# Pass order and operand placement in a split-precision matmul kernel: mirrored passes for the second output tile, second parts one k tile on

## The chip, the cores and the metric

The kernel runs on one core of one Trainium2 chip, as one launch. The metric is device microseconds from the start to the end of an execution; three runs of the kernel before were timed. A profile of one further execution gives each instruction with its start, its end and what it waited for.

## The reference

The reference is two layers of a hybrid block over 256 tokens with 16 learned tokens ahead of them (272 in all), width 1024, in float32. Each layer normalizes, projects to twelve groups of columns, runs three mixers (retention, a gated linear recurrence, differential attention), joins them with gates, and adds a convolutional feed-forward part. A last normalization ends it.

```python
def mixer(hn, w_in, w_branch, w_out, lb, lam_p, subln_g, lambda_init, valid, pos):
    proj = (hn @ w_in).astype(F32)
    rq, rk, rv, rg, hq, hf, hi, hg, dq, dk, dv, mg = jnp.split(proj, offs, axis=-1)
    o_ret = retention(rq, rk, rv, rg, valid, pos)
    o_hg = hgrn2(hq, hf, hi, hg, lb, valid)
    o_da = diff_attention(dq, dk, dv, lam_p, subln_g, lambda_init, valid, pos)
    branches = jnp.stack([o_ret, o_hg, o_da], axis=2)
    y_b = jnp.einsum('blnc,ncd->blnd', branches, w_branch)
    y = jnp.sum(jax.nn.sigmoid(mg) * y_b, axis=2)
    return y @ w_out

def conv_ffn(hn, w_ffn_in, conv_w, conv_b, w_ffn_out, valid):
    u = jnp.where(valid[None, :, None], hn @ w_ffn_in, 0.0)
    up = jnp.pad(u, ((0, 0), (CONV_W - 1, 0), (0, 0)))
    c = conv_b + sum(conv_w[j] * up[:, j:j + l] for j in range(CONV_W))
    gate, val = jnp.split(c, 2, axis=-1)
    return (jax.nn.silu(gate) * val) @ w_ffn_out

for li in range(2):
    h = h + mixer(rms_norm(h, norm_mix_g[li]), ...)
    h = h + conv_ffn(rms_norm(h, norm_ffn_g[li]), ...)
return rms_norm(h, norm_final_g)[:, PAD:]
```

Nearly all arithmetic is in the matrix products with `w_in`, `w_branch`, `w_out`, `w_ffn_in` and `w_ffn_out`.

## The kernel before, in words

**Tiles.** Activations lie with features on the 128 partitions and tokens along the free axis: 272 columns in layer 0, and 258 in most of layer 1 (`t0` = 14 drops tokens that nothing reads any more; the six projections in `FULL` keep 272). Weights are cut on the host into tiles of 128 x 128, in the order of use, and eight tiles make a chunk, `CHUNK_TILES`. A product (`products`, L850) makes two output tiles, `f` = 0 and 1, over the k tiles of its operand: 8, or 22 for `fo`. The k tile is the outer loop and `f` the inner one.

**Two parts.** To get float32 precision out of the single-pass matmul type, every operand is split: `hi` is the operand rounded to that type, `lo` is the rest. A weight tile meets an activation tile in three passes, each a weight load and a matmul into the same PSUM accumulator:

```python
nc.tensor.matmul(o, wh, hi, start=first, stop=False)
nc.tensor.matmul(o, wh, lo, start=False, stop=False)
nc.tensor.matmul(o, wl, hi, start=False, stop=last)
```

These are L873, L874 and L875 of the profile. The weights' split is made on the chip, chunk by chunk, in `_Weights.next` (L577): a DMA from SP's queue brings `wraw`, ScalarE (ACT) writes `whi`, VectorE (DVE) writes `wlo` as the difference. The activations' split is made by `Norm.take` and `Norm.next` (the `x` tiles), by `split_blocks` (`b0` to `b2`), and by `split` (`y` for `wo`, `g` for `fo`).

**Stages.** Names in `ORDER` are projections (`rq` to `m2`, products with `w_in`), `b0` to `b2` (`w_branch`), `wo`, `fi` (`w_ffn_in`, 22 pairs) and `fo`. A pair of output tiles over 8 k tiles is 16 weight tiles and 48 passes. Projections and `fi` stream the `x` tiles, the others stream tiles that lie in slots, buffers of four k tiles each (`SLOTS` of them). In layer 1 `fo` is computed the other way round (`final`, L1351): the weights stream, 512 columns at a time, and the activations are loaded.

**Order.** Everything is recorded first (`_Plan.add`) with a cost and a due time; `_Plan.order` then simulates the engines and buffers, and each engine's instructions are issued in that order. The products keep their program order; small matmuls of the mixers go between them.

**Places.** Addresses within a partition are chosen by hand. `_places` (L127) gives each weight tile its place inside its chunk's buffers, the same in `whi` and `wlo`, by a wanted byte offset modulo `LINE`, 256: 0 for projections in layer 0 (`APART`), 96 for those with 258 columns, another place for every `fi` pair (`SPREAD`), and 64 more for each k tile for `b0` to `b2`, `wo` and `fo`, whose slots hold k tiles 1088 bytes apart. The `x` tiles lie 320 columns (`WIDE`), 1280 bytes, apart, so that all k tiles have the same offset modulo 256. `_runs` turns the places of a chunk into as few ACT and DVE instructions as it can.

Of the kernel before, what the change touches and what calls it, by code (L numbers as in the profile page):

```python
# [11 lines left out]
F32 = mybir.dt.float32  # L12
# [25 lines left out]
SLOTS = 13  # L38
# [47 lines left out]

def _turns(li):

    pairs = [x for x in ORDER if x[0][0] not in MARKS]
    if li == DEPTH - 1:
        pairs = [x for x in pairs if x[0] != "fo"]
    groups = [[x] for x in pairs]
    if li == 0:
        groups[:2] = [pairs[:2]]
    turned = [[x] for n in (BASE, ("fi",)) for x in [x for x in pairs if x[0] in n][DEFER - 1 : DEFER]]
    out = []
    for group in groups:  # L100
        if group == [("fo", 3)]:
            out.append([("fo", 3, k, f) for f in range(2) for k in range(FK)])
        else:
            nk = _ktiles(group[0][0])
            out.append([x + (k, f) for k in range(nk // 2) for x in group for f in range(2)])
            out[-1] += [x + (k, f) for x in group for k in range(nk // 2, nk) for f in range(2)]
# [11 lines left out]
APART = (0, 96)  # L118
# [4 lines left out]
SPREAD = [16 * i for i in range(16)] + [8 + 40 * i for i in range(6)]  # L123
WIDE = 320


def _places(depth=DEPTH):  # L127

    wants = []
    for li in range(depth):
        for name, j, k, _ in sum(_turns(li), []):
            if name == "fo" and (li == DEPTH - 1 or j == 3):
                wants.append(None)
                continue
            short = li == DEPTH - 1 and name not in FULL
            if name in BASE or name == "fi":
                wants.append((SPREAD[j] + 4 * T0 * short if name == "fi" else APART[short]) % LINE)
                continue  # L140
            wants.append(APART[short] + BLOCK * (name[0] == "b" or name in ("wo", "fo")) + 64 * (k % 4))
    out = []
    for c in range(0, len(wants), CHUNK_TILES):
        at, places = 0, []
        for want in wants[c : c + CHUNK_TILES]:
            if want is not None:
                at += (want // 4 - at) % (LINE // 4)
            places.append(at)
            at += P
        assert at <= ROOM  # L150
        out.append(places)
    return out


def _runs(places):


    runs = []
    for i, at in enumerate(places):
        if runs and at == runs[-1][1] + runs[-1][2] * P:  # L160
            runs[-1][2] += 1
        else:
            runs.append([i, at, 1])
    out = []
    for i, at, n in runs:
        if out and out[-1][4] == n and (out[-1][3] == 1 or at == out[-1][1] + out[-1][2] * out[-1][3]):
            if out[-1][3] == 1:
                out[-1][2] = at - out[-1][1]
            out[-1][3] += 1
        else:  # L170
            out.append([i, at, 0, 1, n])
    return out
# [22 lines left out]
def _stream(w_in, w_branch, w_out, w_ffn_in, w_ffn_out):  # L195
# [17 lines left out]
    out = out.reshape(n, CHUNK_TILES, P, P).transpose(0, 2, 1, 3)  # L213
# [349 lines left out]
class _Weights:  # L563
# [9 lines left out]
    def part(self, t, at, step, runs, n):  # L573

        return bass.AP(t.tensor, t.offset + at, [list(t.ap[0]), [max(step, 1), runs], [1, n * P]])

    def next(self):  # L577
        c, i = divmod(self.used, CHUNK_TILES)
        self.used += 1
        if i == 0:  # L580
# [7 lines left out]
            for p in range(pieces):  # L588
                n = CHUNK_TILES // pieces
                cols = slice(p * n * P, (p + 1) * n * P)  # L590
                self.sp.dma_start(raw[:, cols], self.w[c][:, cols])
                for first, at, step, runs, each in _runs(self.places[c][p * n : (p + 1) * n]):
                    src = raw[:, (p * n + first) * P : (p * n + first + runs * each) * P].rearrange("p (r x) -> p r x", r=runs)
                    self.act.activation(self.part(hi, at, step, runs, each), src, AF.Copy)
                    self.dve.tensor_tensor(out=self.part(lo, at, step, runs, each), in0=src, in1=self.part(hi, at, step, runs, each).bitcast(F32), op=SUB)
            self.plan.key = due
            self.cut = hi, lo
        hi, lo = self.cut
        at = self.places[c][i]
        return hi[:, at : at + P], lo[:, at : at + P]  # L600
# [16 lines left out]
def _trace(ctx, tc, plan, a, depth, probe):  # L617
# [232 lines left out]
    def products(xs, name, j, t0=0):  # L850
# [14 lines left out]
        for _, i, k, f in tiles:  # L865
            hi, lo = (x[:, t0:] for x in xs(k))
            begun = left[i, f] < _ktiles(name)
            left[i, f] -= 1
            plan.key = clock[0]
            wh, wl = weights.next()  # L870

            def run(o=to[i, f], wh=wh, wl=wl, hi=hi, lo=lo, first=not begun, last=left[i, f] == 0):
                nc.tensor.matmul(o, wh, hi, start=first, stop=False)  # L873
                nc.tensor.matmul(o, wh, lo, start=False, stop=False)  # L874
                nc.tensor.matmul(o, wl, hi, start=False, stop=last)  # L875

            plan.main.append(plan.add("pe", run, cost, [to[i, f]], [wh, wl, hi, lo]))
            clock[0] += cost
# [26 lines left out]
    def split(hi, lo, x):  # L905
        act.activation(hi, x, AF.Copy)
        tt(lo, x, hi.bitcast(F32), SUB)
# [29 lines left out]

    def split_blocks(name, blocks, t0):

        his, los = [], []  # L940
        for x in blocks:
            hi, lo = slot4(name + "hi", F32R), slot4(name + "lo", F32R)
            split(hi[:, :, t0:], lo[:, :, t0:], x[:, :, t0:])
            his.append(hi)
            los.append(lo)
        return lambda k: (his[k // 4][:, k % 4, :], los[k // 4][:, k % 4, :])

    for li in range(depth):
# [402 lines left out]
        def final():  # L1351
# [21 lines left out]
            for k, t, c in order:  # L1373
# [5 lines left out]
                gh, gl = (x[k // 4][:, k % 4, tokens(t)] for x in (hi, lo))  # L1379
# [27 lines left out]
        for name, j in ORDER:  # L1407
# [88 lines left out]
            elif name in ("b0", "b1", "b2"):  # L1496
# [5 lines left out]
                else:  # L1502
                    tt(g, ps, g, MUL)
                    tt(yy, yy, g, ADD)
                    if name == "b2":
# [3 lines left out]
                        split(st["yhi"][j // 2][:, two, t0:], st["ylo"][j // 2][:, two, t0:], yy)  # L1509
            elif name == "wo":  # L1510
                hi, lo = st["yhi"], st["ylo"]
                ps = products(lambda k: (hi[k // 4][:, k % 4, :], lo[k // 4][:, k % 4, :]), name, j, t0)
# [7 lines left out]
            elif name == "fi":  # L1520
                ps = products(lambda k: x_tile(k, norm.folded), name, j, t0)
                if j % 4 == 0:
                    st.setdefault("ghi", []).append(slot4("ghi", F32R))
                    st.setdefault("glo", []).append(slot4("glo", F32R))
# [4 lines left out]
                first = META if last else 0  # L1529
# [12 lines left out]
                split(st["ghi"][j // 4][:, j % 4, first:], st["glo"][j // 4][:, j % 4, first:], c[:, 0, :])  # L1542
# [3 lines left out]
            else:  # L1546
                hi, lo = st["ghi"], st["glo"]
                ps = products(lambda k: (hi[k // 4][:, k % 4, :], lo[k // 4][:, k % 4, :]), name, j)
# [34 lines left out]
```

## Time and profile before

| | |
|---|---|
| time, median of 3 runs (lowest to highest) | 1326.98 us (1326.49 to 1327.44) |
| the profiled execution: its own time, and its span | 1326.42 us, 1324.6 us |
| mean granted TensorE clock | 0.999 |
| matmuls, weight loads: busy time | 1314.0 us, 1285.7 us |
| DVE, ACT: busy time | 962.4 us, 816.4 us |
| `wraw` loads on SP's queue | 402 of 512 KB and 4 of 256 KB |
| `whi` conversions on ACT, `wlo` on DVE | 408 and 408 |

Times in the profile are microseconds from the span's start, durations of one instruction are nanoseconds. A matmul's row has its start and the time until its result is through the array; since passes overlap, a stream's speed is the distance between starts, not that duration. A row of the timeline has start, duration, engine, line, operation, output<-inputs, and shape.

### The profile page before, as it was taken

What the parts mean: (1) busy time and instruction counts of PE and PEld (TensorE: products, weight loads), DVE (VectorE), ACT (ScalarE), POOL (GpSimd) and SP (SyncE); (2) the same over time, 40 slices, a digit from 0 to 9 for tenths busy, and PEclk for the clock granted to TensorE, in tenths of its full rate; (3) what the DMA queues carried; (4) which work ended last, traced back from release to release, by engine and by line L of the source; (5) the groups of instructions that cost most, each with busy time, mean ns of one, the idle gap of its engine ahead of it and who ended that gap; (6) DMA issues with size and microseconds to landing.
All of it is one profiled execution on the core that took longest, in us unless ns stands there. A gap on an engine that the chain in (4) does not pass through costs nothing.

```text
span 1324.6 us, 28929 instructions
## 1 busy us (share of the span) xinstructions
PE 1314.0 (99%) x11862; PEld 1285.7 (97%) x11862; DVE 962.4 (73%) x1630; ACT 816.4 (62%) x1374; POOL 83.2 (6%) x161
## 2 busy tenths in 40 slices
PE   9999999999999999999999999999999999999998
PEld 8999999999999999999999999999999999999986
DVE  7675777697585789886574757776985867898753
ACT  6847454756576566666456475547565865766643
POOL 5000000001010020000030000000011100200000
PEclk9999999999999999999999999999999999999999
DMA  7544543444544545555555445444445345365653
GB/s 272 194 150 153 172 148 132 140 144 139 181 143 152 183 144 183 183 170 181 175 176 187 149 159 173 148 144 144 148 140 183 136 165 201 131 211 185 204 182 107
DMA packets 60755, 219.07 MB, mean 165 GB/s; under 512 B 6864, under 2 KB 6992, under 8 KB 60624
## 3 DMA queue, kind: packets, MB, share of 16 engines
q1 hardware_dynamic: 60336, 216.71, 48.0%
q8 instruction: 93, 1.52, 0.5%
q10 hardware_dynamic: 288, 0.52, 0.1%
q14 instruction: 38, 0.31, 0.1%
HBM read 216.16 MB, written 1.05 MB: 164 GB/s over the span
## 4 chain that ended last, share of the span: by engine, by line
PE 95%; DVE 3%; ACT 1%; issue 0%; DMA 0%; SPq 0%; DVEq 0%
PE main L873 28%; PE main L875 27%; PE main L874 27%; PE fo L1383 2%; PE fo L1385 2%; PE fo L1384 2%; PE lev L1064 1%; DVE two_b L558 1%; PE ds L1248 1%; PE ms L558 1%; PE do L558 1%; PE ro L558 1%; PE ho L558 1%; PE vt L558 1%; DVE wlo L558 1%; PE s L558 0%
## 5 line engine op out<-in xcount | busy, mean ns | idle before, releaser
L873 PE MATMUL main<-xh,whi 128*128 128x272 f32 (+1 forms) x2368 | 691.8, 292 | 0.7 <-ACT whi L558 0.7
L875 PE MATMUL main<-xh,wlo 128*128 128x272 f32 (+1 forms) x2368 | 676.1, 286 | 1.0 <-DVE wlo L558 0.9
L874 PE MATMUL main<-xl,whi 128*128 128x272 f32 (+1 forms) x2368 | 675.7, 285 | 1.3 <-DVE xl L558 1.3
L558 DVE TENSOR_TENSOR wlo<-wraw,whi 128x1024 fp32r<-128x1024 f32 (+1 forms) x408 | 497.2, 1223 | 197.9 <-ACT whi L558 195.2
L558 ACT ACTIVATE whi<-wraw 128x1024 fp32r<-128x1024 f32 (+1 forms) x408 | 426.4, 1048 | 228.1 <-PE main L874 160.1
L873 PEld LDWEIGHTS main<-xh,whi 128*128 128x128 f32 x2368 | 446.1, 188 | 2.6 <-ACT whi L558 1.1
L874 PEld LDWEIGHTS main<-xl,whi 128*128 128x128 f32 x2368 | 446.1, 188 | 2.3 <-DVE xl L558 1.7
L875 PEld LDWEIGHTS main<-xh,wlo 128*128 128x128 f32 x2368 | 445.7, 188 | 2.4 <-DVE wlo L558 2.3
L558 DVE SCALAR_TENSOR_TENSOR two_b<-main,small,two_b 128x256 f32<-128x256 f32 (+2 forms) x144 | 65.4, 489 | 30.7 <-ACT two_b L558 29.0
L558 ACT ACTIVATE two_b<-main,small 128x272 f32<-128x272 f32 (+1 forms) x72 | 37.2, 566 | 29.6 <-PE main L875 29.6
L558 POOL TENSOR_TENSOR y<-h,rstd 128x272 f32<-128x272 f32 x32 | 34.5, 1113 | 317.7 <-ACT rstd L558 317.7
L875 PE MATMUL main<-ghi,wlo 128*128 128x272 f32 x176 | 51.0, 290 | 0.0
L873 PE MATMUL main<-ghi,whi 128*128 128x272 f32 x176 | 50.9, 289 | 0.0
L874 PE MATMUL main<-glo,whi 128*128 128x272 f32 x176 | 50.2, 285 | 0.0
L558 ACT ACTIVATE vsrc<-main 128x544 f32<-128x544 f32 x24 | 15.0, 625 | 38.5 <-PE main L875 38.4
L873 PE MATMUL main<-b0hi,whi 128*128 128x272 f32 (+1 forms) x128 | 38.2, 298 | 0.0
L873 PE MATMUL main<-b1hi,whi 128*128 128x272 f32 (+1 forms) x128 | 38.1, 298 | 0.0
L875 PE MATMUL main<-b2hi,wlo 128*128 128x272 f32 (+1 forms) x128 | 36.7, 286 | 0.0
L875 PE MATMUL main<-yhi,wlo 128*128 128x272 f32 (+1 forms) x128 | 36.7, 286 | 0.0
L875 PE MATMUL main<-b1hi,wlo 128*128 128x272 f32 (+1 forms) x128 | 36.6, 286 | 0.0
L875 PE MATMUL main<-b0hi,wlo 128*128 128x272 f32 (+1 forms) x128 | 36.6, 286 | 0.0
L873 PE MATMUL main<-b2hi,whi 128*128 128x272 f32 (+1 forms) x128 | 36.5, 285 | 0.0
(244 smaller groups left out, 1934.4 us busy)
## 6 DMA issues: line engine op xcount, KB each, us to landing
wraw<-in_w SPq DMA_DIRECT2D x402, 512.0 KB, 3.3
h<-in_h SPq DMA_DIRECT2D x4, 272.0 KB, 5.7
dec<-in_dec SPq DMA_DIRECT2D x2, 544.0 KB, 5.5
wraw<-in_w SPq DMA_DIRECT2D x4, 256.0 KB, 5.4
const<-in_const SPq DMA_DIRECT2D x1, 937.0 KB, 6.4
gain<-in_gl SPq DMA_DIRECT2D x1, 512.0 KB, 5.2
out<-y ACTq DMA_DIRECT2D x2, 256.0 KB, 2.8
out<-y SPq DMA_DIRECT2D x2, 256.0 KB, 2.7
```

The costliest lines, as they stand in the source:

```text
L558: self.plan.add(self.name, lambda: f(*args, **kw), cost, outs, ins, args[2] if method == "activation" else None)
L873: nc.tensor.matmul(o, wh, hi, start=first, stop=False)
L874: nc.tensor.matmul(o, wh, lo, start=False, stop=False)
L875: nc.tensor.matmul(o, wl, hi, start=False, stop=last)
L1064: nc.tensor.matmul(o, keys, x, start=True, stop=True)
L1248: nc.tensor.matmul(ss[m][:, at : at + nk], q[half, hd, q0 : q0 + P], k[half, hd, :nk], start=True, stop=True)
L1383: nc.tensor.matmul(o, gh, wh, start=False, stop=False)
L1384: nc.tensor.matmul(o, gl, wh, start=False, stop=False)
L1385: nc.tensor.matmul(o, gh, wl, start=False, stop=end)
```

## The change

Six things are changed together.

- **Pass order.** For the second output tile of a k tile (`odd`), the pass `wl`·`hi` comes first instead of last. So the passes of a k tile go hi, lo, hi for the first output tile and hi, hi, lo for the second.
- **Second parts one place on.** The `lo` part of k tile k lies in place (k + 1) % 4 of its tile, for `x` and for every slot. Writes of several k tiles that wrap are made in two pieces (`split`).
- **`x` tiles 272 columns apart** instead of 320 (`WIDE` is gone), so k tiles lie 64 bytes on from each other modulo 256, as in the slots.
- **Weight places.** `_places` gives `whi` and `wlo` places of their own: 64 bytes more per k tile in every stage, one offset for all stages of a width (`APART` is now 64 and 160 bytes, counted from the streamed operand), the second part's place by the operand of the pass that runs before its load. `SPREAD` is gone. Within a chunk the odd tiles are stored first; the host permutes the stream to match.
- **Conversions.** `_boxes` replaces `_runs`: an ACT and a DVE instruction write up to a two-level box of tiles. By the new placement 388 of 404 chunks still take one instruction an engine; ten chunks of `fo` in layer 0 take four, one takes six, five (the first two chunks among them) two.
- **Slots.** 14 instead of 13. In layer 1 the `g` tiles lie 256 columns apart.

```diff
-SLOTS = 13
+SLOTS = 14
...
-APART = (0, 96)
+GROUPED = 4 * KD
+BEGIN = 64
...
-SPREAD = [16 * i for i in range(16)] + [8 + 40 * i for i in range(6)]
-WIDE = 320
+APART = (64, 160)
...
-        for name, j, k, _ in sum(_turns(li), []):
-            if name == "fo" and (li == DEPTH - 1 or j == 3):
+        for i, (name, j, k, _) in enumerate(sum(_turns(li), [])):
+            if name == "fo" and li == DEPTH - 1:
                 wants.append(None)
                 continue
             short = li == DEPTH - 1 and name not in FULL
-            if name in BASE or name == "fi":
-                wants.append((SPREAD[j] + 4 * T0 * short if name == "fi" else APART[short]) % LINE)
-                continue
-            wants.append(APART[short] + BLOCK * (name[0] == "b" or name in ("wo", "fo")) + 64 * (k % 4))
+            apart = APART[short] + 4 * T0 * short - BEGIN + BLOCK * (name not in BASE and name != "fi")
+            turn = 4 * T * (k % 4)
+            lo = apart + turn if i % 2 == 0 else before
+            wants.append([apart + turn, lo + 4 * T * (i % 2 == 0 and len(wants) >= GROUPED)])
+            before = apart + turn
...
+        if c >= GROUPED and None not in mine:
+            order = [i for i in order if i % 2] + [i for i in order if not i % 2]
+            by = [sorted(order, key=lambda i: i ^ 1)] * 2
+            if any(b[0] - a[0] not in (0, 4 * T) for a, b in zip(mine, mine[1:])):
+                by = [sorted(order, key=lambda i: mine[i][part] % LINE) for part in range(2)]
+                order = by[0]
...
+                for first, outer, inner, dims in _boxes(*mine):
+                    src = self.part(raw, (p * n + first) * P, inner * P, P, outer, inner)
+                    to_hi, to_lo = (self.part(t, *x, outer, inner) for t, x in zip((hi, lo), dims))
+                    self.act.activation(to_hi, src, AF.Copy)
+                    self.dve.tensor_tensor(out=to_lo, in0=src, in1=to_hi.bitcast(F32), op=SUB)
...
-    xs = [[fixed([P, KD // 2, WIDE], f"x{n}{i}", F32R)[:, :, :T] for n in "hl"] for i in range(3)]
+    xs = [[fixed([P, KD // 2, T], f"x{n}{i}", F32R) for n in "hl"] for i in range(3)]
...
-        return tuple(t[:, k % 4, :] for t in xs[1 if k >= 4 else 2 if folded else 0])
+        return tuple(t[:, (k + n) % 4, :] for n, t in enumerate(xs[1 if k >= 4 else 2 if folded else 0]))
...
-                nc.tensor.matmul(o, wh, hi, start=first, stop=False)
-                nc.tensor.matmul(o, wh, lo, start=False, stop=False)
-                nc.tensor.matmul(o, wl, hi, start=False, stop=last)
+                passes = [(wh, hi), (wh, lo)]
+                passes.insert(0 if odd else 2, (wl, hi))
+                for n, (w, x) in enumerate(passes):
+                    nc.tensor.matmul(o, w, x, start=first and n == 0, stop=last and n == 2)
...
-    def split(hi, lo, x):
+    def split(hi, lo, x, k):
+
         act.activation(hi, x, AF.Copy)
-        tt(lo, x, hi.bitcast(F32), SUB)
+        n = hi.shape[1]
+        for a, b in ((0, min(n, 3 - k)), (min(n, 3 - k), n)):
+            if a < b:
+                to = (k + a + 1) % 4
+                tt(lo[:, to : to + b - a], x[:, a:b], hi[:, a:b].bitcast(F32), SUB)
```

More of the change, by code (lines that the diff above doesn't have):

```diff
@@ L142, in _places @@
+            wants.append([apart + turn, lo + 4 * T * (i % 2 == 0 and len(wants) >= GROUPED)])
+            before = apart + turn
     out = []
     for c in range(0, len(wants), CHUNK_TILES):
[L144 to L151, printed above, removed]
-    return out
[L155 to L171, printed above, removed]
+        mine = wants[c : c + CHUNK_TILES]
@@ new lines, in _places @@
+        order, places = list(range(CHUNK_TILES)), [[0] * CHUNK_TILES for _ in range(2)]
+        by = [order, order]
+        if c >= GROUPED and None not in mine:
[4 more added lines that the diff above has]
+                order = by[0]
```

84 lines of the change are left out of this document (58 added, 26 removed).

## The prediction

> **What bounds the kernel now.** I read the page's busy table first, then the chain that ended last, then the costliest groups.
>
> ```profile
> span 1324.6 us, 28929 instructions
> PE 1314.0 (99%) x11862; PEld 1285.7 (97%) x11862; DVE 962.4 (73%) x1630; ACT 816.4 (62%) x1374; POOL 83.2 (6%) x161
> ...
> PE 95%; DVE 3%; ACT 1%; issue 0%; DMA 0%; SPq 0%; DVEq 0%
> ...
> L873 PE MATMUL main<-xh,whi 128*128 128x272 f32 (+1 forms) x2368 | 691.8, 292 | 0.7 <-ACT whi L558 0.7
> ...
> L873 PEld LDWEIGHTS main<-xh,whi 128*128 128x128 f32 x2368 | 446.1, 188 | 2.6 <-ACT whi L558 1.1
> ```
>
> TensorE is busy for 1314.0 of 1324.6 us and 95% of the chain is its own, so the time is the number of passes (one weight load and one matmul) times the distance from one pass's start to the next. The 292 ns in the group's row is one pass from issue to drain; passes overlap, so the distance must be read from start times. The profiled execution took 1326.42 us, 1.8 us more than its span, and the median of the three runs is 1326.98; I work against the profile and carry the difference over to the median.
>
> Start to start is not constant. In the timeline I took the first pass of a stretch and the first pass of what follows it, and divided by the passes between (48 to each pair of output tiles, by program order).
>
> ```profile
> 44.30 0.29 PE L873 MATMUL main<-xh,whi 128*128 128x272 f32 x1
> 67.98 0.29 PE L873 MATMUL main<-xh,whi 128*128 128x272 f32 x1
> ...
> 559.27 0.29 PE L873 MATMUL main<-xh,whi 128*128 128x272 f32 x1
> 565.34 0.29 PE L873 MATMUL main<-xh,whi 128*128 128x272 f32 x1
> ...
> 685.92 0.28 PE L873 MATMUL main<-xh,whi 128*128 128x272 f32 x1
> 709.61 0.29 PE L873 MATMUL main<-xh,whi 128*128 128x258 f32 x1
> 732.24 0.28 PE L873 MATMUL main<-xh,whi 128*128 128x272 f32 x1
> ...
> 1157.67 0.28 PE L873 MATMUL main<-xh,whi 128*128 128x258 f32 x1
> 1163.47 0.28 PE L873 MATMUL main<-xh,whi 128*128 128x258 f32 x1
> 1169.07 0.29 PE L873 MATMUL main<-xh,whi 128*128 128x258 f32 x1
> ```
>
> The first two rows bound the four `hg` pairs of layer 0: 23.68 us over 192 passes, 123.33 ns. The next two bound one `fi` pair of the same shape, the fifteenth: 6.07 us over 48, 126.5 ns. `hf` of layer 1, again 272 columns, takes 123.4; `hg` of layer 1, 258 columns, 22.63 us over 192, 117.9. In layer 1 the sixth `fi` pair takes 120.8 and the seventh 116.7 (5.80 and 5.60 us over 48). Same instruction, same shape, same neighbours, and up to 4 ns between one pair and the next.
>
> What differs is the addresses. Call *relation* the place of the weights that the next pass loads minus the place of the operand that this pass streams, in bytes modulo 256. In the program as it stands the `x` tiles start at 0, the weight chunks at 64 and the slots at 64 (mod 256). `SPREAD` gives each `fi` pair a place of its own, so the `fi` stage is a table of relations. At 272 columns, 64 gives 123.3 (`hg`, `hf`) and 32 gives 126.5 (the fifteenth pair). At 258 columns, 104 gives 117.9 (`hg`), 144 gives 120.8 and 160 gives 116.7. These two, 64 and 160, are the relations that the changed code sets everywhere but in the last stage.
>
> The Trainium skill says otherwise: "TensorE: Matmul & The Clock Gate", section "Step-by-step: what each phase is for", gives TensorE two independent read ports, so that loading the next weights takes no bandwidth from the running matmul. By it no address matters and the change leaves the time where it is; the 126.5 against 123.3 ns speak against it here, and it stands as a rival below.
>
> **The change part by part.** I worked the relations out from the diff. In a pair of tiles the passes now go: wh0·hi, wh0·lo, wl0·hi, wl1·hi, wh1·hi, wh1·lo, then the next k tile. With `x` at 272 columns (1088 bytes, 64 mod 256) k tile k sits 64k on, its second part 64(k+1) on; the first parts of the weights sit 64k on, and the second parts 64k+64 (first output tile) or 64k (second one). All six transitions then have the same relation: 64 at 272 columns, 160 at 258. Before, stages with slots as operands (`b0`-`b2`, `wo`, `fo`) had it in five of six, with 64 more at the step to the next k tile.
>
> *What the new steady state costs.* The stretches whose operands all lie at one place take, per six passes, 740.0 ns (`hg`, layer 0), 707.2 (`hg`, layer 1) and 700 (seventh pair): 111, 106 and 105 times 6.67 ns. Where each k tile lies 64 bytes on, the layer 0 rows below give 748.1 per six (192 passes in 23.94 us), which is 112 such steps and a quarter. I estimate that an orderly run of the new layout ends on a whole step and a quarter too: 741.7 ns per six at 272 columns (123.6 a pass) and 701.7 at 258 (116.9).
>
> ```profile
> 449.56 0.29 PE L873 MATMUL main<-yhi,whi 128*128 128x272 f32 x1
> 473.50 0.28 PE L873 MATMUL main<-xh,whi 128*128 128x272 f32 x1
> ...
> 510.75 0.29 PE L873 MATMUL main<-xh,whi 128*128 128x272 f32 x1
> 607.62 0.29 PE L873 MATMUL main<-ghi,whi 128*128 128x272 f32 x1
> 657.00 0.29 PE L873 MATMUL main<-ghi,whi 128*128 128x272 f32 x1
> ...
> 1103.61 0.28 PE L873 MATMUL main<-yhi,whi 128*128 128x258 f32 x1
> 1126.59 0.28 PE L873 MATMUL main<-xh,whi 128*128 128x258 f32 x1
> ...
> 1249.62 0.28 PE L873 MATMUL main<-xh,whi 128*128 128x258 f32 x1
> 1257.12 0.39 PE L1383 MATMUL fo<-whi,ghi 128*128 128x512 f32 x1
> 1317.84 0.40 PE L1385 MATMUL fo<-wlo,ghi 128*128 128x512 f32 x1
> ```
>
> The sum, in passes times nanoseconds:
>
> 1. `fi`, layer 0, last 16 pairs (510.75 to 607.62): 126.1 now, 768 × 2.5 = −1.9 us.
> 2. `b0`, `b1`, `b2`, `wo`, layer 0, at the rate of `wo` (449.56 to 473.50, 124.7): 768 × 1.1 = −0.8.
> 3. `fo`, layer 0 (607.62 to 657.00, 396 passes, 124.7): 528 × 1.1 = −0.6.
> 4. The 30 projection pairs with 258 columns: at least 1440 × 0.9 (the `hg` rate, 117.9) = −1.3, at most 1440 × 2.8 (if they ran like `wo`) = −4.0. I take −2.0, nearer to `hg`, which runs the very operands; stages broken up by other matmuls cannot always hold that rate.
> 5. `b0`-`b2` and `wo`, layer 1 (1103.61 to 1126.59 over 192, 119.7): 768 × 2.8 = −2.1.
> 6. `fi`, layer 1, last 17 pairs, at the rate of sixteen of them (1157.67 to 1249.62 over 768, 119.7): 816 × 2.8 = −2.3.
> 7. Projections with 272 columns: 74 pairs, 3552 passes, already at relation 64, pay the quarter step: + 0.28 each = +1.0.
> 8. The last stage, 512 columns (1257.12 to 1317.84 over 263 starts, 230.9): four relations become one, 0. The two are untested; the spread between relations at 272 columns is 2.6%, half of it is 0.8 us of these 61 either way.
>
> I take nothing for the first pairs of `fi` in both layers, where VectorE sets the pace:
>
> ```profile
> 1127.00:1155.00 28.00, 26.68 (x221) 26.39 (x221) 24.78 (x39) 22.06 (x36) 8.63 (x8) 1.00 0.39 135
> 1155.00:1254.00 99.00, 99.00 (x826) 99.00 (x825) 85.33 (x147) 67.21 (x107) 0.00 (x0) 1.00 0.59 197
> 610.00:673.00 63.00, 63.00 (x505) 62.92 (x504) 35.25 (x43) 29.46 (x37) 0.00 (x0) 1.00 0.51 180
> ...
> PE main L874 <- DVE xl L558: 1.3, 1, 1.3
> ...
> L558 DVE TENSOR_TENSOR wlo<-wraw,whi 128x1024 fp32r<-128x1024 f32 x400 | 491.0, 1232 | 194.2 <-ACT whi L558 191.7 <-PE main L875 1.7
> L558 DVE TENSOR_TENSOR wlo<-wraw,whi 128x256 fp32r<-128x256 f32 x1 | 0.4, 424 | 1.1 <-ACT whi L558 1.1
> ```
>
> In windows the columns are stretch, its length, then busy time of PE, PEld, DVE, ACT, POOL. From 1127 to 1155 us PE lacks 1.3 us, which is the one wait for `xl`; a faster PE there only waits longer. After that DVE has 85.33 of 99 us; with passes 2.8 ns shorter the stretch is 2.3 us shorter and DVE stands at 88%, still behind PE.
>
> *What is added on other engines.* The placements give 36 more conversion pieces, nearly all in `fo` of layer 0, each on ACT and on DVE. A quarter chunk takes 424 ns where a quarter of 1232 is 308, so about 0.12 us a piece, 4 us of DVE in a stage that uses 35.25 of 63. Hidden; were PE to wait for every piece it would be 4 us. The wrapped write of the second parts splits 16 DVE subtractions in two, 2 us of DVE over the whole kernel, behind passes. The loads keep their number and size, so SP's queue does not change. In the first 32 tiles the second parts are not turned; I put +0.1 us for that. The fourteenth slot can only free the planner; PE waits for no slot now, so 0.
>
> Sum: −1.9 −0.8 −0.6 −2.0 −2.1 −2.3 +1.0 +0.1 = −8.6 us. The profile would read 1317.8 us and the median 1318.4.
>
> **The rivals.** *One step more.* If runs with moving operands cannot end on the smallest step, every aligned six takes 6.67 ns more, as `wo` of layer 0 does now: 124.7 and 118.1. Then item 7 becomes 3552 × 1.4 = +5.0, items 2 and 3 vanish, the others shrink to −1.1, −0.4, −1.3 and −1.4: +0.9 with the first tiles, 1327.9. For it: the only rows in which k tiles are 64 apart run at this rate. Against: those rows have a foreign relation in every sixth pass, which by itself could cost a step.
>
> *Own weights count (slower).* The change keeps the distance to the next weights but alters a pass's distance to its own: now equal in all passes, then 0 in the second and sixth and 128 in the third. If that distance matters as much as the other, half the passes move to a bad relation: half of 126.5 − 123.3 at 272 columns, +1.6, and half of 120.8 − 116.7 at 258, +2.1, over the rates above. Item 7 becomes 3552 × 1.9 = +6.6; items 1, 2, 3: −0.7, +0.4, +0.3; item 4 turns to +1.0; 5 and 6 to −0.5 and −0.6. Together +6.5 us, 1333.5. It decides once the 272-column projections exceed about 125.7 ns. No stretch varies that distance alone, so nothing excludes it. Against it, a weight load runs beside the pass before its own:
>
> ```profile
> 402.39 0.28 PE L873 MATMUL main<-xh,whi 128*128 128x272 f32 x1
> 402.39 0.19 PEld L874 LDWEIGHTS main<-xl,whi 128*128 128x128 f32 x1
> 402.51 0.29 PE L874 MATMUL main<-xl,whi 128*128 128x272 f32 x1
> ```
>
> The load for the pass that starts at 402.51 starts with the one at 402.39, so the operand it can meet is that one's.
>
> *Addresses do nothing*, the rule of the two ports: 1327.0. The pairs in the first fence, alike but for their places, speak against it.
>
> *Half of it*: one width reaches its small step and the other does not. With the step at 258 columns alone the sum is −5.3 (1321.7), at 272 alone −2.4 (1324.6).
>
> **How the numbers follow.** Forecast with its neighbourhood (1312 to 1321) 0.60, half of it 0.15, one step more 0.10, own weights 0.11, addresses nothing 0.04. The measurement can tell about 0.2%, 2.6 us, from no change: faster than 1324.3 holds the first and most of the second, 0.73; the same holds the rest of it, the step and the ports, 0.16; slower is the fourth, 0.11. The range reaches down by the lower ends of items 4 and 8 and the uncounted first pairs of `fi` (−2.0, −0.8, −0.9, and as much again for a step less at one width), to 1311.5, and up to the one-step case, 1328; what is left out is the slower rival and little else.
>
> **What would show it.** Right: `hg` of layer 0 at 123.3 to 123.9 ns a pass, `hg` and all `fi` pairs of layer 1 at 116.7 to 117.3 and alike, `wo` of layer 0 no longer slower than `hg`, 36 more `wlo` pieces. Wrong: 272-column projections at 124.7 or more, `fi` pairs that still differ, or PE idle before `wlo` in `fo`.

## The result and the profile after

The changed kernel is slower: 1332.51 us median (1331.98 to 1332.98, six runs) against 1326.57 (1326.30 to 1327.44, six runs) of the kernel before on the same chip, ratio 1.0046 with the 95% interval 1.0036 to 1.0056. The profiled execution has a span of 1331.0 us, 6.4 more than before, at a granted clock of 0.999 as before. The forecast was 1318.4.

The page of the changed kernel, its busy line, its chain and the groups that answer to those shown of before:

```profile
span 1331.0 us, 29023 instructions
PE 1320.1 (99%) x11862; PEld 1293.1 (97%) x11862; DVE 965.4 (73%) x1682; ACT 821.3 (62%) x1410; POOL 80.1 (6%) x161
...
PE 93%; DVE 4%; ACT 1%; DMA 1%; issue 1%; SPq 0%; DVEq 0%; ACTq 0%
...
L588 DVE TENSOR_TENSOR wlo<-wraw,whi 128x1024 fp32r<-128x1024 f32 (+4 forms) x444 | 498.6, 1134 | 207.5 <-ACT whi L588 206.2
L907 PE MATMUL main<-xh,whi 128*128 128x272 f32 (+1 forms) x2368 | 644.3, 289 | 0.0
```

TensorE is still the bound, with the same 11862 matmuls, and busy 6.1 us longer. The 36 extra conversion pieces are there (444 against 408), and DVE and ACT are 3.0 and 4.9 us busier. Passes simply start further apart. The view of PE's waits has nothing that could hold 6 us (the two groups of TensorE's main passes are shown):

```profile
PE main L907 <- DVE wlo L588: 1.5, 3, 1.1
PE main L907 <- DVE xl L588: 1.4, 1, 1.4
```

Before, they were 0.9 and 1.3 us.

The timeline gives the distances, by the first pass of a stretch and the first pass of what follows. All three passes of a tile have one line now, L907.

```profile
44.88 0.29 PE L907 MATMUL main<-xh,whi 128*128 128x272 f32 x1
68.94 0.29 PE L907 MATMUL main<-xh,whi 128*128 128x272 f32 x1
...
528.28 0.29 PE L907 MATMUL main<-xh,whi 128*128 128x272 f32 x1
606.80 0.29 PE L907 MATMUL main<-xh,whi 128*128 128x272 f32 x1
612.84 0.28 PE L907 MATMUL main<-ghi,whi 128*128 128x272 f32 x1
662.42 0.28 PE L907 MATMUL main<-ghi,whi 128*128 128x272 f32 x1
691.41 0.29 PE L907 MATMUL main<-xh,whi 128*128 128x272 f32 x1
715.57 0.28 PE L907 MATMUL main<-xh,whi 128*128 128x258 f32 x1
738.46 0.29 PE L907 MATMUL main<-xh,whi 128*128 128x272 f32 x1
...
1182.91 0.28 PE L907 MATMUL main<-xh,whi 128*128 128x258 f32 x1
1257.28 0.28 PE L907 MATMUL main<-xh,whi 128*128 128x258 f32 x1
1264.75 0.39 PE L1423 MATMUL fo<-whi,ghi 128*128 128x512 f32 x1
1324.36 0.39 PE L1425 MATMUL fo<-wlo,ghi 128*128 128x512 f32 x1
```

`hg` of layer 0 (44.88 to 68.94, 192 passes) went from 123.3 to 125.3 ns a pass, `hf` of layer 1 (691.41 to 715.57), by the code at the same relation, from 123.4 to 125.8, `hg` of layer 1 (715.57 to 738.46) from 117.9 to 119.2. The `fi` pairs are now alike, as forecast, but at the wrong speed: pairs 8 to 20 of layer 0 (528.28 to 606.80, 624 passes) take 125.8, those of layer 1 (1182.91 to 1257.28) 119.2. In the mean that is nearly what they took before, 125.8 and 119.8; before, the single pairs of layer 0 among them lay between 123.6 and 127.7. `fo` has 125.2 over 396 passes (was 124.7). Only the last stage gained: 59.61 us over 263 starts, 226.7 ns against 230.9.

### The profile page after: what moved, and what is told of

Same layout as the page of the kernel before. It is cut to its first block, busy times and chain, and to the rows that moved or that the text cites. A ratio compares the mean times of both kernels' runs of the same rounds, so it can differ in the third digit from the quotient of the medians.

```text
span 1331.0 us, 29023 instructions
## 1 busy us (share of the span) xinstructions
PE 1320.1 (99%) x11862; PEld 1293.1 (97%) x11862; DVE 965.4 (73%) x1682; ACT 821.3 (62%) x1410; POOL 80.1 (6%) x161
## 4 chain that ended last, share of the span: by engine, by line
PE 93%; DVE 4%; ACT 1%; DMA 1%; issue 1%; SPq 0%; DVEq 0%; ACTq 0%
PE main L907 80%; PE fo L1424 2%; PE fo L1423 2%; PE fo L1425 1%; PE lev L1104 1%; DVE two_b L588 1%; DVE wlo L588 1%; PE ds L1288 1%; PE do L588 1%; PE ms L588 1%; DVE xl L588 1%; PE ro L588 1%; PE ho L588 1%; PE vt L588 1%; ACT whi L588 0%
## 5 line engine op out<-in xcount | busy, mean ns | idle before, releaser
L588 DVE TENSOR_TENSOR wlo<-wraw,whi 128x1024 fp32r<-128x1024 f32 (+4 forms) x444 | 498.6, 1134 | 207.5 <-ACT whi L588 206.2
L907 PE MATMUL main<-xh,whi 128*128 128x272 f32 (+1 forms) x2368 | 644.3, 289 | 0.0
L907 PE MATMUL main<-xl,whi 128*128 128x272 f32 (+1 forms) x2368 | 639.9, 287 | 1.5 <-DVE xl L588 1.4
L588 ACT ACTIVATE whi<-wraw 128x1024 fp32r<-128x1024 f32 (+4 forms) x444 | 430.6, 979 | 245.9 <-PE main L907 172.2
L907 PE MATMUL main<-xh,wlo 128*128 128x272 f32 (+1 forms) x2368 | 503.3, 289 | 1.7 <-DVE wlo L588 1.5
L907 PEld LDWEIGHTS main<-xl,whi 128*128 128x128 f32 x2368 | 446.2, 188 | 2.4 <-DVE xl L588 2.2
L907 PEld LDWEIGHTS main<-xh,whi 128*128 128x128 f32 x2368 | 446.5, 189 | 1.0
L907 PEld LDWEIGHTS main<-xh,wlo 128*128 128x128 f32 x2368 | 378.2, 189 | 3.9 <-DVE wlo L588 3.2
L907 PE MATMUL main<-glo,whi 128*128 128x272 f32 x176 | 47.7, 289 | 0.0
L907 PE MATMUL main<-ghi,whi 128*128 128x272 f32 x176 | 47.1, 287 | 0.0
L907 PE MATMUL main<-ghi,wlo 128*128 128x272 f32 x176 | 36.8, 290 | 0.0
L907 PE MATMUL main<-b1hi,whi 128*128 128x272 f32 (+1 forms) x128 | 35.4, 292 | 0.0
L907 PE MATMUL main<-b0hi,whi 128*128 128x272 f32 (+1 forms) x128 | 35.1, 290 | 0.0
L907 PE MATMUL main<-b1lo,whi 128*128 128x272 f32 (+1 forms) x128 | 34.7, 286 | 0.0
L907 PE MATMUL main<-b0lo,whi 128*128 128x272 f32 (+1 forms) x128 | 34.6, 286 | 0.0
L1423 PE MATMUL fo<-whi,ghi 128*128 128x512 f32 x88 | 34.2, 389 | 0.0
L1424 PE MATMUL fo<-whi,glo 128*128 128x512 f32 x88 | 34.2, 389 | 0.0
```

Of the source, the lines that this page charges most:

```text
L588: self.plan.add(self.name, lambda: f(*args, **kw), cost, outs, ins, args[2] if method == "activation" else None)
L907: nc.tensor.matmul(o, w, x, start=first and n == 0, stop=last and n == 2)
L1423: nc.tensor.matmul(o, gh, wh, start=False, stop=False)
L1424: nc.tensor.matmul(o, gl, wh, start=False, stop=False)
```

## Experiments

Rates below are those of `fi` pairs 8 to 20 (624 passes) in layer 0 (272 columns) and layer 1 (258), unless another stage is named. "Next" is the prediction's relation (weights of the next pass minus this pass's operand, modulo 256), "own" the same with a pass's own weights. Both are worked out from the code: a trace holds no addresses. "Six passes" are those of one k tile, three for each output tile.

**The order alone.** The kernel before, with the mirrored order for the second output tile and nothing else.

```diff
+                passes = [(wh, hi), (wh, lo)]
+                passes.insert(0 if odd else 2, (wl, hi))
```

> The kernel before with the mirrored pass order alone; every address as before. Theory OWN (the weights' place counts against the operand of the pass they are loaded for as well, not only against the operand that streams during the load) and theory SHIFT (it costs when the streamed operand changes its place from one pass to the next): no address moves, so 1326.6 us within 0.2%, hg of layer 0 at 123.3 ns a pass. Theory ORDER (the new order itself costs): most of the loss is here, 272-column projections near 125.5 ns, 1332 us.

1327.62 us, ratio 1.0008 (0.9998 to 1.0017), with `hg` of layer 0 at 123.3 ns a pass as before. With the operands where they were, the order costs nothing that can be told.

**Second parts in place.** The changed kernel, with both parts of a k tile at the same place again. Order, k tiles 64 bytes apart, `APART`, 14 slots and the layout of the last stage stay.

```diff
-            wants.append([apart + turn, lo + 4 * T * (i % 2 == 0 and len(wants) >= GROUPED)])
+            wants.append([apart + turn, apart + turn])
-        return tuple(t[:, (k + n) % 4, :] ...
+        return tuple(t[:, k % 4, :] ...
```

> The changed kernel with the second parts of operands and weights put back beside the first (not one place on); k tiles still 64 bytes on, order still mirrored. Distance to the own weights is 64 (160) in every pass, to the next weights too except 128 (224) at the step to the next k tile. OWN: all 272-column stages run like wo of the kernel before, 124.7 ns, the slow pass is the one before the step; projections lose 3552 x 1.2 = 4.3 us against before, fi of layer 0 gains 0.9, the 258-column stages fall between 116.7 and 119.7; 1325 to 1331 us, and less than the changed kernel's 1332.5. SHIFT: one change of place in six passes instead of four, so a quarter of the loss, about 123.9 ns and 1326 to 1328 us. ORDER: no better than 1332.

```profile
525.56 0.29 PE L905 MATMUL main<-xh,whi 128*128 128x272 f32 x1
603.39 0.29 PE L905 MATMUL main<-xh,whi 128*128 128x272 f32 x1
...
1181.62 0.28 PE L905 MATMUL main<-xh,whi 128*128 128x258 f32 x1
1255.98 0.28 PE L905 MATMUL main<-xh,whi 128*128 128x258 f32 x1
```

1331.63 us, ratio 1.0041 (1.0026 to 1.0056). The two stretches give 124.7 and 119.2 ns: k tiles that step 64 bytes cost 1.4 and 2.5 ns a pass against operands in one place (next experiment) although every pass keeps its own distance and only one next relation in six differs. The 124.7 is what the theory OWN gave, though the total lies 0.6 us above its range; SHIFT, with 123.9, is off.

**One relation a width, operands in one place.** The kernel before with only its weight places changed; `x` stays 320 columns apart, the order is the old one.

```diff
-                wants.append((SPREAD[j] + 4 * T0 * short if name == "fi" else APART[short]) % LINE)
+                wants.append((APART[short] + 4 * T0 * short) % LINE)
-            wants.append(APART[short] + BLOCK * (...) + 64 * (k % 4))
+            wants.append(APART[short] + 4 * T0 * short + BLOCK * (...) + 64 * (k % 4))
```

> The kernel before with nothing but its weight places changed: all fi pairs and all projections of a width have one relation, 64 at 272 columns and 160 at 258; x tiles stay 320 columns apart, order and second parts as before. OWN and SHIFT: all distances equal in all passes and no operand moves, so 123.3 ns and 116.7 ns in projections and fi: fi of layer 0 -2.3 us, 258-column projections -2.0, fi of layer 1 -3.0, together -7.3, about 1319.3 us. If the 116.7 ns of one fi pair was an accident of its surroundings: 258-column stages stay at 118 to 119.5, about 1323 us.

```profile
523.33 0.29 PE L873 MATMUL main<-xh,whi 128*128 128x272 f32 x1
600.29 0.29 PE L873 MATMUL main<-xh,whi 128*128 128x272 f32 x1
...
1171.97 0.28 PE L873 MATMUL main<-xh,whi 128*128 128x258 f32 x1
1244.78 0.28 PE L873 MATMUL main<-xh,whi 128*128 128x258 f32 x1
```

1321.36 us, ratio 0.9962 (0.9947 to 0.9977), with 123.3 and 116.7 ns. So 64 and 160 are good values, and giving them to every pass of the projections and of `fi` is a gain, as long as the operands don't move. (`b0` to `b2`, `wo` and `fo` keep k tiles that step 64 bytes.)

**The second weight part displaced, operands in one place.** In `fi`, `wlo` lies 16 j bytes on in pair j; next then differs in the second pass of a tile, own in the third. (The last six pairs, and `b0` to `b2` and `wo`, try other places with both parts alike.)

```diff
+                move = 16 * j * part if j < 16 else EXTRA[li][j - 16]
+                wants.append((APART[short] + 4 * T0 * short + move) % LINE)
```

> The kernel of one relation per width (64 and 160), in which fi pair j (j below 16) has its second weight parts wl displaced by 16 j bytes; streamed operands all at one place, passes in the old order hi, lo, hi. So in pass 2 only the distance to the next weights is displaced, in pass 3 only the distance to its own weights. (fi pairs from 16 on displace all weights by other amounts, and b0 to b2 and wo take 16 relations in turn: a scan.) Theory NEXT (the one of the prediction: only the weights loaded during a pass count): pass 2 slows and pass 3 does not, and the mean of a pair lies a third of the way from 123.3 to what that relation took in the kernel before, e.g. 124.4 for pair 14 (126.5 in all passes there: relation 32). OWN: pass 3 slows as much as pass 2 or more, pair 14 at 125 or above. SHIFT alone says nothing against NEXT here.

```profile
530.11 0.29 PE L883 MATMUL main<-xh,whi 128*128 128x272 f32 x1
536.19 0.29 PE L883 MATMUL main<-xh,whi 128*128 128x272 f32 x1
542.17 0.29 PE L883 MATMUL main<-xh,whi 128*128 128x272 f32 x1
```

One timed run, 1326.79 us, so the pairs are compared with each other. These rows bound pairs 9 and 10 of layer 0 (`wlo` at 208 and 224): 126.7 and 124.5. In layer 0 the undisplaced pair has 123.5, the other fifteen 124.3 to 126.7, distances of 140 ns or over, where PE waits, left out. Which pass loses varies: in pair 1 the third takes 130.2 in the mean (132 once settled) and the second 125.3, in pair 3 they take 126.3 and 128.2 (start-to-start distances). That a third pass slows, whose next relation is as before, speaks against the prediction's premise that only the next relation counts; that only the own one does isn't shown either. In `b0` to `b2` and `wo` of layer 1, place 208 took 118.3 ns, 160 took 119.3.

**The second parts alone.** The kernel of the third experiment, with `xl` and the `wlo` tiles that meet `x` 64 bytes on. Next stays constant, own becomes 64, 0, 128 (160, 96, 224); no k tile moves.

```diff
-                wants.append((APART[short] + 4 * T0 * short) % LINE)
+                wants.append((APART[short] + 4 * T0 * short + 64 * part) % LINE)
-    xs = [[fixed([P, KD // 2, WIDE], f"x{n}{i}", F32R)[:, :, :T] for n in "hl"] for i in range(3)]
+    xs = [[... [:, :, 16 * (n == "l") : 16 * (n == "l") + T] ...
```

> The kernel with one relation a width (1321.4 us; 123.3 ns a pass in the fi stage of layer 0, 116.7 in layer 1), in which only the second parts of x and of the weights that meet x are moved on by 64 bytes. The distance to the weights that the next pass loads stays 64 (160) in every pass; the distance of a pass to its own weights becomes 64, 0, 128 (160, 96, 224) instead of constant; no k tile is moved. Theory that the own distance counts: 4608 passes at 272 columns go from 123.3 to 125.2 ns (+8.8 us) and 2496 at 258 from 116.7 to about 119 (+5.7): 1335.9 us. Rival, that only the step from k tile to k tile costs (the kernel with the second parts in place and the k tiles 64 bytes on reads 124.6 and 119.2): nothing moves, 123.3 and 116.7, 1321.4 us.

```profile
525.83 0.29 PE L877 MATMUL main<-xh,whi 128*128 128x272 f32 x1
604.18 0.29 PE L877 MATMUL main<-xh,whi 128*128 128x272 f32 x1
...
1179.10 0.28 PE L877 MATMUL main<-xh,whi 128*128 128x258 f32 x1
1252.59 0.28 PE L877 MATMUL main<-xh,whi 128*128 128x258 f32 x1
```

1330.24 us, ratio 1.0029 (1.0019 to 1.0040); 125.6 and 117.8 ns. The next relation is the same in every pass and the rate is not, so the premise falls. At 272 columns this alone costs 2.2 ns a pass, nearly all that the changed kernel lost against 123.3; at 258 only 1.1 of 2.5. With next held constant, own moves exactly when the operand's place does, so "the own distance counts" and "the operand must stay" can't be parted here. Both edits of the change cost, and not by addition (this run has the old order): 1.4 and 2.2 ns alone, 2.5 together at 272; 2.5 and 1.1 alone, 2.5 together at 258.

**Other steps from k tile to k tile.** The kernel of the second experiment with `x` 304 or 288 columns apart (192 or 128 bytes on modulo 256), weights following, and 13 slots.

```diff
-            turn = 4 * T * (k % 4)
+            turn = 4 * (WIDE if (name in BASE or name == "fi") and len(wants) >= GROUPED else T) * (k % 4)
```

> The kernel with second parts in place, in which the x tiles lie 304 columns apart, so that k tiles (and the weights that meet them) step 192 bytes, that is 64 back modulo 256, instead of 64 on; 13 slots; the own distance stays constant, the next one is foreign (0, or 96 at 258) once in six. Theory that the start of a pass is tied to its operand's place, 1.67 ns for 64 bytes, and six passes end on whole steps of 6.67 ns plus that: six passes end a quarter short of a step, 738.3 or 745.0 ns (123.1 or 124.2 a pass) at 272 columns, 698.3 or 705.0 (116.4 or 117.5) at 258; about 1317 to 1325 us. Rival, that one foreign relation in six costs a step whatever it is: 124.6 and 119.2 again, 1331.6 us. Second rival, only the own distance counts: 123.3 and 116.7, about 1320 us.

```profile
524.11 0.29 PE L906 MATMUL main<-xh,whi 128*128 128x272 f32 x1
601.59 0.29 PE L906 MATMUL main<-xh,whi 128*128 128x272 f32 x1
...
1175.22 0.28 PE L906 MATMUL main<-xh,whi 128*128 128x258 f32 x1
1248.54 0.28 PE L906 MATMUL main<-xh,whi 128*128 128x258 f32 x1
```

> The same with x tiles 288 columns apart: k tiles step 128 bytes, the next relation is foreign (192, or 32 at 258) once in six. Theory of the tied start: six passes end half a step on, 743.3 or 750.0 ns (123.9 or 125.0 a pass) at 272 columns, 703.3 or 710.0 (117.2 or 118.3) at 258; about 1323 to 1331 us. Rival, a foreign relation costs a step whatever it is: 124.6 and 119.2, 1331.6 us. Second rival, only the own distance counts: 123.3 and 116.7, about 1320 us.

```profile
1176.90 0.28 PE L906 MATMUL main<-xh,whi 128*128 128x258 f32 x1
1250.04 0.28 PE L906 MATMUL main<-xh,whi 128*128 128x258 f32 x1
```

304: 1324.06 us, ratio 0.9982 (0.9973 to 0.9991); six passes take 705.0 ns at 258 columns, as foreseen from the tied start. At 272 they take 742 and 748 ns in turn from one k tile to the next; the 745.0 that was foreseen is met by the mean alone. 288: 1326.60, 1.0002 (0.9993 to 1.0011); 703.3 at 258 columns, as foreseen, but at 272 six passes take 740 and 753 ns in turn, 746.6 in the mean, which was not. So a foreign next relation once in six has no fixed price: it changes with the step, and why each step costs what it does isn't shown.

**Two places more.** The kernel of the third experiment, with `g` of layer 1 256 columns apart (as in the changed kernel) and `b0` to `b2` and `wo` of layer 1 at 208.

```diff
-                gh, gl = (x[k // 4][:, k % 4, tokens(t)] for x in (hi, lo))
+                gh, gl = (x[k // 4][:, k % 4, t * P : (t + 1) * P] for x in (hi, lo))
-            ... + BLOCK * (name[0] == "b" or name in ("wo", "fo")) + 64 * (k % 4))
+            ... + (BLOCK + 48 * short) * (name[0] == "b" or name in ("wo", "fo")) + 64 * (k % 4))
```

> The kernel with one relation a width (1321.4 us) with two places more: the g tiles of layer 1 lie 256 columns apart, so that the last stage has one relation, 0, and should run at the 226.7 ns of the kernel after instead of 230.9 (264 passes, -1.1 us); b0 to b2 and wo of layer 1 go to relation 208, which took 118.3 in the scan instead of 119.3 (768 passes, -0.8 us). If both hold alone as they did in their kernels: 1319.5 us. If the last stage gained from something else in the kernel after (the second parts, the order, the 14 slots): 1320.6.

```profile
1251.09 0.39 PE L1383 MATMUL fo<-whi,ghi 128*128 128x512 f32 x1
1310.71 0.39 PE L1385 MATMUL fo<-wlo,ghi 128*128 128x512 f32 x1
```

1319.09 us, ratio 0.9945 (0.9932 to 0.9959). The last stage takes 226.7 ns a pass with nothing else of the change, so its gain comes from the `g` tiles 256 columns apart (by the code, four relations become one, 0).

**A scan of relations in the changed layout.** The changed kernel, with weights of `fi` pair j 16 j bytes further on.

```diff
+            apart += (16 * j if j < 16 else EXTRA[j - 16]) * (name == "fi")
```

> The changed kernel, in which only the fi stage differs: pair j of each layer has its weights (both parts) 16 j bytes further on, so that its next-load relation is 64 + 16 j (layer 0) or 160 + 16 j (layer 1) for j up to 15, and 72, 88, 104, 136, 168, 216 (168, 184, 200, 232, 8, 56) for the last six. Everything else stays. Theory that 64 and 160 were only the wrong values for operands that move: some pairs fall to 123.9 ns a pass or less in layer 0 and to 117.2 or less in layer 1, against 125.8 and 119.2 at 64 and 160. Theory that moving the operands costs by itself: no pair comes under 124.5 in layer 0 or 117.9 in layer 1, whatever its place. Total time between 1329 and 1336 us by either, so the pairs' own rates are to be read.

```profile
528.75 0.29 PE L909 MATMUL main<-xh,whi 128*128 128x272 f32 x1
534.70 0.29 PE L909 MATMUL main<-xh,whi 128*128 128x272 f32 x1
540.78 0.29 PE L909 MATMUL main<-xh,whi 128*128 128x272 f32 x1
...
1246.47 0.28 PE L909 MATMUL main<-xh,whi 128*128 128x258 f32 x1
1252.13 0.28 PE L909 MATMUL main<-xh,whi 128*128 128x258 f32 x1
1257.90 0.28 PE L909 MATMUL main<-xh,whi 128*128 128x258 f32 x1
```

One timed run, 1333.54 us. Pairs 8 and 9 of layer 0 (192 and 208) take 5.946 and 6.086 us unrounded over 48 passes, 123.9 and 126.8 ns; pairs 19 and 20 of layer 1 (232 and 8) take 118.0 and 120.4. In the scan 80 and 192 are the best at 272 columns, both 123.9, and 64 reads 125.6; at 258 columns the best is 232, over 1 ns above the 116.7 of operands in one place. This is one execution, with one pair for each value.

**The changed kernel at these relations.**

```diff
-APART = (64, 160)
+APART = (192, 232)
```

> The changed kernel with one line altered: the relations are 192 at 272 columns and 232 at 258 instead of 64 and 160, the best of the scan in the changed layout (123.9 and 118.0 ns a pass in fi, against 125.7 and 119.2 of the changed kernel). Theory that the change failed by these two values: every stage goes to about 123.9 and 118.0; by the passes of the changed kernel that is 3275 projection passes x 1.55 = -5.1, b0-b2 and wo of layer 0 721 x 1.5 = -1.1, fi 1048 x 1.8 = -1.9, fo 526 x 1.5 = -0.8, 258-column projections 1317 x 1.25 = -1.6, b0-b2 and wo of layer 1 700 x 1.15 = -0.8, fi 1046 x 1.2 = -1.3: -12.6 us, 1319.9 us. Rival, that the good value belongs to a stage and its neighbours and not to the layout: the gain stays in fi, -3.2 us, 1329.3 us.

```profile
44.96 0.29 PE L907 MATMUL main<-xh,whi 128*128 128x272 f32 x1
68.91 0.29 PE L907 MATMUL main<-xh,whi 128*128 128x272 f32 x1
...
525.01 0.29 PE L907 MATMUL main<-xh,whi 128*128 128x272 f32 x1
602.14 0.29 PE L907 MATMUL main<-xh,whi 128*128 128x272 f32 x1
...
608.08 0.29 PE L907 MATMUL main<-ghi,whi 128*128 128x272 f32 x1
624.41 0.28 PE L907 MATMUL main<-ghi,whi 128*128 128x272 f32 x1
640.87 0.29 PE L907 MATMUL main<-ghi,whi 128*128 128x272 f32 x1
657.33 0.29 PE L907 MATMUL main<-ghi,whi 128*128 128x272 f32 x1
...
1174.73 0.28 PE L907 MATMUL main<-xh,whi 128*128 128x258 f32 x1
1248.40 0.28 PE L907 MATMUL main<-xh,whi 128*128 128x258 f32 x1
```

1324.02 us, ratio 0.9979 (0.9969 to 0.9988), between the two expectations: one line turns the change from slower to faster than before. `fi` reaches 123.6 ns (741.7 for six passes, the very figure forecast for 64) and 118.1. But `hg` at the same relation takes 124.7, so a value doesn't carry from stage to stage either. It doesn't even hold within a stage. The four rows at 608.08 to 657.33 bound the first three pairs of `fo`, 132 passes each: 123.7, 124.7 and 124.7 ns. Within each pair next and own distances are the same by the code; past the first six, the first pair holds 741 or 742 ns for six passes, the others 748 or 749. One arrangement thus has two steady lengths, 6.7 ns apart. What makes a stretch take one or the other isn't shown; the second pair starts after a single foreign relation, where the k tiles begin again.

**A joined version.** Mirrored order, `x` in one place at 64 and 160, only the slots with second parts one place on, at 192 and 232; 13 slots, `g` of layer 1 256 columns apart.

```diff
+            moved = name not in BASE and name != "fi"
+            apart = (MOVED if moved else APART)[short] + ...
+            turn = 4 * T * (k % 4) * moved
```

> A joined version: mirrored order; x and its weights in one place at 64 and 160, both parts alike (123.3 and 116.7 to 117.5 ns a pass, as measured); only the slots keep the second parts one place on, at relations 192 and 232; 13 slots; g of layer 1 256 columns apart. Against the best kernel so far (1319.1 us) the slot stages change: b0-b2 and wo of layer 0 from 124.6 to 123.9 (-0.5 us), fo from 125.0 to 123.9 (-0.6), b0-b2 and wo of layer 1 from 118.2 to 118.0 (-0.2): 1317.8 us. Rival, the good value belongs to a stage: 1319.1 or a little over.

1318.49 us, ratio 0.9932 (0.9918 to 0.9945): the fastest kernel run here, though its interval overlaps that of the version at 0.9945. It lies between its two expectations: `wo` of layer 0 reaches 123.6, but the first three pairs of `fo` stay at 124.7, where 123.9 was expected.

## Why the prediction was wrong

The account in us against before, from the traces: for each kind of stage the sum of all distances from one matmul's start to the next. The forecast's items stand beside it. "K tiles step, parts in place" is the second experiment, "second parts alone" the one of that name, "neither" the third; in these last two only projections and `fi` are rearranged, and the slots are laid out as before.

| stage (item) | forecast | after | k tiles step, parts in place | second parts alone | neither | after at 192, 232 |
|---|---|---|---|---|---|---|
| `fi`, layer 0 (1) | −1.9 | +0.2 | −0.7 | −0.2 | −1.8 | −1.6 |
| `b`, `wo`, layer 0 (2) | −0.8 | +0.5 | 0.0 | 0.0 | 0.0 | −0.3 |
| `fo`, layer 0 (3) | −0.6 | +0.2 | −0.2 | 0.0 | 0.0 | −0.2 |
| projections, 258 (4) | −2.0 | +1.0 | +3.7 | −0.3 | −1.3 | −0.3 |
| `b`, `wo`, layer 1 (5) | −2.1 | −0.2 | +0.5 | +0.4 | +0.3 | −0.9 |
| `fi`, layer 1 (6) | −2.3 | −0.4 | −0.3 | −1.6 | −2.5 | −1.2 |
| projections, 272 (7) | +1.0 | +6.1 | +3.4 | +4.6 | +0.1 | +3.3 |
| last stage (8) | 0 | −1.1 | −1.1 | 0.0 | 0.0 | −1.1 |
| first tiles, small matmuls | +0.1 | +0.3 | +0.1 | 0.0 | +0.3 | +0.1 |
| sum | −8.6 | +6.5 | +5.2 | +2.9 | −5.0 | −2.4 |

*What held.* TensorE's pace was the bound, no other engine came in, the conversion pieces were 36 and hidden: no wait of PE stands in `fo` of layer 0. By the code of `_places` the relations are 64 and 160 in all but a few passes where a stage or pair begins, as worked out from the diff, and the later `fi` pairs of each layer became alike.

*The step that failed* is "What the new steady state costs": a layout with moving operands would end a quarter step above the rate that one place has at the same relation. In `fi` six passes take 755 and 715 ns instead of 741.7 and 701.7: two steps and a quarter above 740 and 700, not a quarter. Nor is the fraction always a quarter: `hg` and `wo` of layer 0 take 751.7, which is 112 steps and three quarters. Behind it stood the premise that a rate belongs to the next relation alone. The 123.3 and 116.7 were read from stretches in which own and next were equal and operands stood still; the change took both away. The estimate of a whole step and a quarter rested on one stage, `wo`, whose second parts lay in place. Moving the second parts alone (125.6 at 272 columns) and stepping the k tiles alone (119.2 at 258) show that one of the two is enough for nearly all of the loss at a width. It fell hardest on item 7, the 3552 passes that were already at relation 64 and, in `hg` and `hf`, ran at 123.3: +6.1 instead of +1.0. The stages that were to gain 9.7 us together in items 1 to 6 lost 1.3.

*Item 8* was sized 0 ± 0.8 and gained 1.1: one relation instead of four is worth 4.2 ns on a 512-column pass.

*The rivals.* "Own weights count" gave 1333.5 with 125.2 and 119.0; measured were 1332.5, 125.3 to 125.8 and 119.2, and its mark, 272-column projections over 125.7 ns, is met by `hf` (125.8) and missed by `hg` (125.3). Its number came close; its mechanism isn't shown. At 272 columns the second parts alone (125.6) fit it, but the operand's move would do as well. At 258 it gave 119.0, while the second parts alone make 117.8 and the step of the k tiles, which leaves own constant, makes 119.2 by itself. Nor is an own distance of 0 bad in itself: at relation 192 it occurs too, and `fi` runs at 123.6. "One step more" gave 124.7 at 272, what k tiles that step have by themselves; its reason, that moving operands cannot end on the smallest step, falls with the 741.7 at 192. "Addresses do nothing" falls with every pair of rows above. The two read ports that the Trainium skill describes ("TensorE: Matmul & The Clock Gate", "Step-by-step: what each phase is for") would by themselves leave all these kernels alike; the traces disagree, by 740 against 755 ns for six passes of the same instructions.

*The evidence against the slower rival* was that the load beside a pass is that of the next one. The overlap is in the rows, but it doesn't show that a pass is free of its own weights' place, and no stretch of the kernel before varied own alone.

*Open:* why 192 suits moving operands and 64 suits standing ones; whether the own distance or the operand's move is what costs; and what picks one of two steady lengths at the same places, as in `fo` at 192, which may also be why `hg` and `fi` differ by 1.1 ns there. The 258-column projections with parts in place lost 3.7 us. They have 76 more distances of 140 ns or over than before, and 74 of these are 140 ns exactly, up to five in a row: not waits of varying length but another steady pace, 21 steps to a pass, whose cause is open.

## What to carry to other kernels

A rate that was read under one arrangement is a property of the whole arrangement; before carrying it to a layout that changes two distances, run one stage in the new layout, scanned over its free offset, as `SPREAD` had done for the old one. Where passes are paced by operand places, keep the streamed operands of consecutive passes at one offset and tune the weights to it; if they must move, choose the offset anew, and expect that one stage's best value may fail in the next. A change that makes many slow passes equal to few fast ones should be costed first on the passes that are already fast, for they have nothing to gain.

## What the hardware showed

Many stretches settle on a fixed length for six passes with loads, and lengths of one kind differ by whole steps of 6.67 ns (706.7 against 700.0, 755.0 against 748.3). With the streamed first parts of all k tiles at one offset modulo 256, 740.0, 753.3, 700.0 and 706.7 were seen, whole numbers of steps. With k tiles 64 bytes on, 748.3, 755.0, 741.7, 715.0 and 708.3 were seen, a quarter over. At 258 columns 192 bytes gave 705.0 (three quarters) and 128 gave 703.3 (a half).

This is a tendency, not a rule. At 272 columns the steps 192 and 128 give two lengths in turn (742 and 748, 740 and 753). In the changed kernel, `hg` and `wo` of layer 0 take 751.7 although k tiles step 64 bytes; and pairs 11 and 13 of `fi` in layer 0 of the kernel before take 750.0 in the mean with operands at one place, half a step over. Which whole number a stretch settles on isn't a matter of offsets alone: at 192 one stage ran at 741.7 and then at 748.3 with the same offsets.
